# Modulating in place in PSUM, Newton steps with scalar operands, and the residual's affine step from the last tile on

## The chip, the cores and the metric

The kernel runs on one core of one Trainium2 chip. Its engines work side by side, each through its own queue of instructions in a fixed order: PE (TensorE) does matmuls and transposes into PSUM, DVE (VectorE) and ACT (ScalarE) work element by element on SBUF and PSUM, POOL (GpSimd) does element work on SBUF and issues some DMAs, and SP (SyncE) issues most DMAs. The metric is the device time of one execution in microseconds (us); less is better.

## The reference, cut to what matters

Two layers run over 640 tokens of width 1024: 512 latent tokens and 128 context tokens. Each layer is

```python
shift1, scale1, gate1, shift2, scale2, gate2 = jnp.split(mod.astype(x.dtype), 6, axis=-1)
u = x * (1 + scale1) + shift1
q_c, kv_c, k_r, p_in, g_b, g_c, h_in = split_cols(u @ w_in, IN_SIZES)
...   # latent attention, pooling mixer, gated convolution
mix = jnp.concatenate([a_out, b_out, c_out], axis=-1) @ w_out
x = layer_norm(ALPHA * x + gate1 * mix, ln1_g, ln1_b)
u = x * (1 + scale2) + shift2
x = layer_norm(ALPHA * x + gate2 * expert_choice_ffn(u, w_router, w_gate, w_up, w_down), ln2_g, ln2_b)
```

`layer_norm` takes mean and variance over the 1024 columns of a token. The last line of layer 0 and the first three of layer 1 are the boundary that most of this change is about.

## The kernel before, in words

**Tiles.** The tokens are five tiles of 128 rows: t = 0 to 3 latent, t = 4 (`CTX`) context. Weights are read from HBM in float32; a float32 product is made of three matmuls (`mm3`, lines 229 to 232: high by high, high by low, low by high), so every operand is first split into a high part, rounded by a CAST on ACT (`...h`), and a low part, the difference, made on DVE or POOL (`...l`): `split`, lines 225 to 227.

**Stages.** Layer 0: adaLN modulation, combined input projection (column groups A, B, P, GC, H, GB, which accumulate in the PSUM tiles `ps_a`, `ps_b` and `ps_c`), attention and the other mixers, output projection, layer norm, routing, 16 experts in pairs, layer norm; then layer 1 the same. The experts read 6 MB of weights each.

**The boundary between the layers** (`finish`, line 1444 on, called for each tile in turn). A tile's sum stands in two PSUM halves `ps_z`. `ln_stats` takes bn_stats of both halves (L312) and their aggregate (L300); then 1/sqrt(variance + eps) is made. With `dve` true that is `rsqrt_dve`: a first guess by integer arithmetic and three Newton steps, each one `tensor_scalar` (L295) and one `scalar_tensor_tensor` (L296), all on 128x1 values on DVE. With `dve` false it is `rsqrt`: one `tensor_scalar` on DVE (L284) and one power on POOL (L285). Before, all five tiles of the boundary take the Newton form. Then DVE makes `nb` = -mean times that value (L1450), and ACT writes the normalised tile `z` from PSUM in two activations (L1452).

`build_uT` turns `z` into the next layer's input: in two halves g = 0, 1, PE transposes four 128x128 blocks into one PSUM bank `tr8` (L253; two such banks exist, pool `ptr`), `modulate` multiplies and adds per partition, two slices of four on DVE (L264) and two on ACT (L261), into an SBUF tile `umod`, and `split` makes `uTh` (CAST, L226) and `uTl` (difference, L227) of `umod`. The A and B projections of layer 1 multiply `uTh` and `uTl`.

`keep` (line 1472) then turns each `z` into the residual that layer 1 needs later: POOL multiplies by `ln_g` and adds `ln_b` (`affine`, L337 and L338) in place, and issues the store to `xres` (L1477). These are put behind `following["split"]`, a split of weights, in the order of issue.

**What sets the order.** The program is written stage by stage, and a list scheduler orders the instructions of each engine by its own model of times; `tc.issue_after(x)` puts what follows behind x in that order, and `tc.high_priority()` ahead of the rest. So an edit in one place can move rows of an engine far from it. On the chip each engine then follows its own list in order: an instruction whose inputs are late holds back all that stand behind it.

The same `build_uT` starts layer 0 with the tiles of x, with `umod` in the `xhalf` tiles; `zero_pads` uses one more such tile.

## Time and profile before

| | |
|---|---|
| median of three runs | 1296.16 us (1294.45, 1296.16, 1302.5) |
| the profiled execution | 1294.52 us |
| its span (first to last instruction) | 1292.7 us |
| PE busy | 1193.2 us, 92% of the span |
| DVE, ACT, POOL busy | 543.7, 368.3, 252.8 us |
| mean granted TensorE clock | 0.966 |

The profiled execution lies 1.64 us under the median, and 1.8 us of it lie outside its span. A timeline row gives the start of an instruction, its length, its engine, line, operation and tiles, and in brackets how long the engine was idle before it and what ended that. A row "x8" puts eight instructions together. Matmuls are pipelined: a row's length is longer than its distance to the next.

### The profile page before, as it was taken

The numbers are of one execution on the slowest core, as the hardware profiler recorded it, in microseconds if no ns is written. First come the engines' busy times: TensorE is split into PE (matmuls) and PEld (weight loads), VectorE is DVE, ScalarE is ACT, GpSimd is POOL, SyncE is SP. The second block draws the span as 40 slices with busy tenths as digits, with TensorE's granted clock in tenths as the row PEclk, the third lists the DMA queues.
The fourth block names the chain that finished last, engine by engine and source line by source line (L and its number), as shares of the span: only waits on it lengthen the run. The fifth ranks groups of instructions, "written<-read, shape, count | busy, mean of one in ns | idle before, by whom it ended". The sixth has DMA issues, their size and how long they took to land.

```text
span 1292.7 us, 18180 instructions
## 1 busy us (share of the span) xinstructions
PE 1193.2 (92%) x7244; PEld 710.7 (55%) x7244; DVE 543.7 (42%) x1266; ACT 368.3 (28%) x800; POOL 252.8 (20%) x234
## 2 busy tenths in 40 slices
PE   5999999999879999999969999999987999999994
PEld 1877886987523333333349998798752333333331
DVE  1554464777531121111297756477653111111116
ACT  1532134663411110111145423475341101011111
POOL 0210002004330221121175000200433022012114
PEclk8999999999979999999989999999998999999998
DMA  9868666164869999999543315606487999999932
GB/s 360 310 209 301 226 237 226 69 214 150 339 259 402 397 396 406 410 400 332 193 138 98 86 46 197 242 19 225 157 320 287 406 396 396 410 406 386 357 102 82
DMA packets 85078, 342.34 MB, mean 265 GB/s; under 512 B 18713, under 2 KB 32089, under 8 KB 54401
## 3 DMA queue, kind: packets, MB, share of 16 engines
q1 hardware_dynamic: 73568, 305.96, 61.4%
q0 software_dynamic: 9840, 29.45, 8.4%
q10 hardware_dynamic: 1584, 5.77, 1.1%
q8 instruction: 57, 0.93, 0.3%
q14 instruction: 29, 0.23, 0.1%
HBM read 313.73 MB, written 27.51 MB: 264 GB/s over the span
## 4 chain that ended last, share of the span: by engine, by line
PE 84%; DVE 7%; ACT 4%; DMA 2%; issue 1%; SPq 1%; POOL 0%; POOLq 0%; ACTq 0%; DVEq 0%
PE ps_d L239 9%; PE ps_g L239 9%; PE ps_u L239 9%; PE ps_gc L239 8%; PE ps_dc L239 5%; PE ps_ada L185 4%; PE ps_c L230 3%; PE ps_c L232 3%; PE ps_c L231 3%; PE ps_o L231 3%; PE ps_o L230 3%; PE ps_o L232 3%; PE ps_p L733 1%; PE tr L239 1%; PE ps_b L230 1%
## 5 line engine op out<-in xcount | busy, mean ns | idle before, releaser
L239 PE MATMUL ps_g<-wg,xT 128*64 128x512 f32 x512 | 116.1, 595 | 0.1
L239 PE MATMUL ps_d<-wd,hT 128*64 128x512 f32 x512 | 113.6, 595 | 2.5 <-DVE yc L1184 1.6
L239 PE MATMUL ps_u<-wu,xT 128*64 128x512 f32 x512 | 115.4, 592 | 0.0
L239 PE MATMUL ps_gc<-wu,xc 128*32 128x512 f32 x512 | 115.0, 595 | 0.0
L239 PE MATMUL ps_gc<-wg,xc 128*32 128x512 f32 x512 | 115.0, 594 | 0.0
L1161 ACT ACTIVATE sc<-ps_gc 32x512 f32<-32x512 f32 x32 | 18.8, 587 | 328.8 <-PE ps_gc L239 299.7
L1163 DVE TENSOR_TENSOR hc<-ps_gc,sc 32x512 f32<-32x512 f32 x32 | 22.0, 688 | 174.9 <-ACT sc L1161 174.8
L239 PEld LDWEIGHTS ps_d<-wd,hT 128*64 128x64 f32 x512 | 35.5, 137 | 78.7 <-issue 75.7
L1110 POOL DMA_INDIRECT yaccc<-yc,csi x28 | 39.8, 1421 | 192.5 <-DVE yc L1184 155.0
L239 PEld LDWEIGHTS ps_g<-wg,xT 128*64 128x64 f32 x512 | 36.0, 137 | 75.1 <-issue 72.7
L239 PEld LDWEIGHTS ps_u<-wu,xT 128*64 128x64 f32 x512 | 37.2, 137 | 72.6 <-issue 71.8
L239 PE MATMUL ps_dc<-wd,hcT 128*32 128x512 f32 x512 | 71.1, 705 | 0.9 <-ACT hcT L1172 0.9
L239 PEld LDWEIGHTS ps_gc<-wg,xc 128*32 128x32 f32 x512 | 29.2, 110 | 75.0 <-issue 73.7
L185 PE MATMUL ps_ada<-wada,cs 128*32 128x512 f32 x368 | 60.1, 630 | 4.8 <-DMA wada<-in_w_ada_dram 4.8
L1212 DVE SCALAR_TENSOR_TENSOR ye<-ps_d,lg,gl 128x512 f32<-128x512 f32 x32 | 24.0, 751 | 95.7 <-PE ps_d L239 92.9
L1191 DVE TENSOR_TENSOR h<-ps_u,sg 128x512 f32<-128x512 f32 x16 | 11.1, 692 | 104.1 <-PE ps_u L239 104.1
L261 ACT ACTIVATE xT<-tr,modB,modA 128x128 f32<-128x128 f32 x64 | 28.0, 459 | 60.8 <-DVE xT L264 59.1
L239 PEld LDWEIGHTS ps_dc<-wd,hcT 128*32 128x32 f32 x512 | 17.2, 126 | 43.0 <-issue 39.1
L961 POOL DMA_INDIRECT xsl<-zrow,lgi x16 | 15.9, 991 | 102.3 <-PE tr L239 87.9
L285 POOL TENSOR_TENSOR bsd<-bsd,neg_half 128x1 f32<-128x1 f32 x15 | 9.5, 634 | 128.7 <-DVE bsd L284 128.7
L1184 DVE SCALAR_TENSOR_TENSOR yc<-ps_dc,cg,gc 128x512 f32<-128x512 f32 x16 | 12.0, 749 | 52.9 <-PE ps_dc L239 52.9
L227 POOL TENSOR_TENSOR wo00l<-r_wo,wo00h 128x1024 fp32r<-128x1024 f32 x4 | 10.4, 2610 | 119.4 <-ACT wo00h L226 119.4
(618 smaller groups left out, 2839.0 us busy)
## 6 DMA issues: line engine op xcount, KB each, us to landing
wg<-in_w_gate_dram SPq DMA_DIRECT2D x64, 1024.0 KB, 12.4
wu<-in_w_up_dram SPq DMA_DIRECT2D x64, 1024.0 KB, 14.9
wd<-in_w_down_dram SPq DMA_DIRECT2D x64, 1024.0 KB, 17.8
wada<-in_w_ada_dram SPq DMA_DIRECT2D x46, 1024.0 KB, 7.2
r_wo<-in_w_out_dram SPq DMA_DIRECT2D x8, 1024.0 KB, 8.7
zrow<-xa ACTq DMA_DIRECT2D x8, 512.0 KB, 7.7
yacc<-xa POOLq DMA_DIRECT2D x8, 512.0 KB, 9.9
z<-yacc SPq DMA_DIRECT2D x8, 512.0 KB, 6.2
```

Source lines behind the costliest of these rows:

```text
L185: nc.tensor.matmul(ps[32 * j:32 * j + 32, :], lhsT=cs[:, k, :], rhs=w[:, j * 512:(j + 1) * 512], start=(k == 0), stop=(k == KD - 1))
L230: nc.tensor.matmul(out, lhsT=lh, rhs=rh, start=first, stop=False)
L231: nc.tensor.matmul(out, lhsT=lh, rhs=rl, start=False, stop=False)
L232: nc.tensor.matmul(out, lhsT=ll, rhs=rh, start=False, stop=last)
L239: line["pe"] = op(*args, **kw)
L261: nc.scalar.activation(out=out[:, kk, :], in_=ps[:, kk, :], func=AF.Identity, scale=A[:, r, k:k + 1], bias=B[:, r, k:k + 1])
L733: nc.tensor.transpose(pt[:, kk, i * P:(i + 1) * P], prs[i][:, (k0 + kk) * P:(k0 + kk + 1) * P], ident)
L961: ins = nc.gpsimd.indirect_dma_start(out=x, out_offset=None, in_=src, in_offset=bass.IndirectOffsetOnAxis(ap=idx, axis=0))
L1110: nc.gpsimd.indirect_dma_start(out=acc[:, :], out_offset=bass.IndirectOffsetOnAxis(ap=idx[h][0:64, j:j + 1], axis=0), in_=y[hs], in_offset ...
L1161: nc.scalar.activation(out=sc[64 * i + 32:64 * i + 64], in_=pc[64 * i:64 * i + 32], func=AF.Silu)
L1163: nc.vector.tensor_tensor(out=hc[32 * i:32 * i + 32], in0=pc[64 * i + 32:64 * i + 64], in1=sc[64 * i + 32:64 * i + 64], op=ALU.mult)
L1212: order["ye"] = nc.vector.scalar_tensor_tensor(out=ye[:, hs], in0=pd, scalar=lg[:, j:j + 1], in1=gl2[:, hs], op0=ALU.mult, op1=ALU.mult)
```

## The change

`build_uT` has no `umod` tile any more: `modulate` writes in place in the PSUM bank that the transposes filled, and `split` reads that bank. A bank is thus held until its `uTl` is made. Between the layers the second half gives three slices of four to ACT and one to DVE. The Newton step and `nb` become `tensor_scalar` with scalar operands. Tiles 2, 3 and 4 of the boundary take the power on POOL. `keep` runs from the last tile to the first, each tile behind the store of the one before it.

```diff
--- before.py
+++ after.py
@@ -264,15 +264,14 @@
                 nc.vector.tensor_scalar(out=out[:, kk, :], in0=ps[:, kk, :], scalar1=A[:, r, k:k + 1],
                                         scalar2=B[:, r, k:k + 1], op0=ALU.mult, op1=ALU.add)
 
-    def build_uT(t, xn, uTh, uTl, A, B, newhalf, ready=None):
+    def build_uT(t, xn, uTh, uTl, A, B, ready=None, on_act=((1, 3), (1, 3))):
         r = 1 if t == CTX else 0
 
         def emit(g, ps):
             ks = slice(4 * g, 4 * g + 4)
-            u = newhalf("umod").rearrange("p (k n) -> p k n", k=4)
-            modulate(u, ps, A, B, r, g)
+            modulate(ps, ps, A, B, r, g, on_act[g])
             tok = slice(t * P, (t + 1) * P)
-            split(uTh[:, ks, tok], uTl[:, ks, tok], u)
+            split(uTh[:, ks, tok], uTl[:, ks, tok], ps)
         if ready is None:
             transpose8(xn, emit)
         else:
@@ -293,7 +292,7 @@
         nc.vector.tensor_scalar(out=y.bitcast(I32), in0=xe.bitcast(I32), scalar1=-0.5, scalar2=0x5f3759df, op0=ALU.mult, op1=ALU.add)
         for _ in range(3):
             nc.vector.tensor_scalar(out=t, in0=y, scalar1=y[:, 0:1], scalar2=xh, op0=ALU.mult, op1=ALU.mult)
-            nc.vector.scalar_tensor_tensor(out=y, in0=t, scalar=1.5, in1=y, op0=ALU.add, op1=ALU.mult)
+            nc.vector.tensor_scalar(out=y, in0=t, scalar1=1.5, scalar2=y[:, 0:1], op0=ALU.add, op1=ALU.mult)
 
     def ln_final(stt, dve):
         mv = st([P, 2], "bmv")
@@ -319,7 +318,7 @@
                                     op0=ALU.subtract, op1=ALU.mult)
         else:
             nb = st([P, 1], "bnb")
-            nc.vector.scalar_tensor_tensor(out=nb, in0=mv[:, 0:1], scalar=-1.0, in1=sd, op0=ALU.mult, op1=ALU.mult)
+            nc.vector.tensor_scalar(out=nb, in0=mv[:, 0:1], scalar1=sd[:, 0:1], scalar2=-1.0, op0=ALU.mult, op1=ALU.mult)
             nc.scalar.activation(out=z, in_=z, func=AF.Identity, scale=sd[:, 0:1], bias=nb[:, 0:1])
 
     def xin(t):
@@ -1406,9 +1405,9 @@
     for t in range(NT):
         if t == 0:
             with tc.high_priority():
-                build_uT(t, x0, *mp[4], A, B, xhalf, early)
+                build_uT(t, x0, *mp[4], A, B, early)
         else:
-            build_uT(t, xin0(t), *mp[4], A, B, xhalf)
+            build_uT(t, xin0(t), *mp[4], A, B)
     cpool("psf")
     with tc.issue_after(order["u"].ins):
         load_tables()
@@ -1444,14 +1443,14 @@
         def finish(t, ps, L2, newrow, newhalf):
             z = newrow("z", "crow" if t == CTX else "row")
             with tc.high_priority() if l + 1 == depth else ExitStack():
-                mv, sd = ln_stats(ps, l + 1 < depth)
+                mv, sd = ln_stats(ps, l + 1 < depth and t < 2)
             if l + 1 < depth or t < 3:
                 nb = st([P, 1], "bnb")
-                nc.vector.scalar_tensor_tensor(out=nb, in0=mv[:, 0:1], scalar=-1.0, in1=sd, op0=ALU.mult, op1=ALU.mult)
+                nc.vector.tensor_scalar(out=nb, in0=mv[:, 0:1], scalar1=sd[:, 0:1], scalar2=-1.0, op0=ALU.mult, op1=ALU.mult)
                 for n in range(2):
                     nc.scalar.activation(out=z[:, n * 512:n * 512 + 512], in_=ps[n], func=AF.Identity, scale=sd[:, 0:1], bias=nb[:, 0:1])
             if l + 1 < depth:
-                build_uT(t, z, *following["mp"][4], *following["AB"], newhalf)
+                build_uT(t, z, *following["mp"][4], *following["AB"], on_act=((1, 3), (1, 2, 3)))
                 following["z"].append((t, z))
             else:
                 c = 640
@@ -1471,10 +1470,11 @@
 
         def keep(L2):
 
-            for t, z in following["z"]:
-                with tc.issue_after(following["split"].ins):
+            prev = following["split"] if following["z"] else None
+            for t, z in following["z"][::-1]:
+                with tc.issue_after(prev.ins):
                     affine(L2, z, z)
-                nc.gpsimd.dma_start(out=xres[t * P:(t + 1) * P, :], in_=z)
+                    prev = nc.gpsimd.dma_start(out=xres[t * P:(t + 1) * P, :], in_=z)
 
         experts(l, A, B, ctxr, ln, gates, newrow, newhalf, late, xc, route_late, ps_dn, preload, start_next, finish, keep)
         if l + 1 < depth:
```

Three places show how rows move. First PE, where the transposes of tile 1 (`z_5294`) and tile 2 (`z_5347`) meet the first matmuls of layer 1's projection A for tile 0 (`ps_a_5569`). Before:

```order
L253 MATMUL tr8_5315<-ident_72,z_5294 128x128 x4
L253 MATMUL tr8_5327<-ident_72,z_5294 128x128 x4
L253 MATMUL tr8_5368<-ident_72,z_5347 128x128 x4
L253 MATMUL tr8_5380<-ident_72,z_5347 128x128 x4
L230 MATMUL ps_a_5569<-wA10h_5219,uTh1_5217 128x384
L231 MATMUL ps_a_5569<-wA10l_5220,uTh1_5217 128x384
```

After (line numbers of the changed file, one lower from `rsqrt` on), with tile 1 as `z_5282` and tile 0's sum as `ps_a_5525`:

```order
L253 MATMUL tr8_5303<-ident_72,z_5282 128x128 x4
L253 MATMUL tr8_5314<-ident_72,z_5282 128x128 x4
L230 MATMUL ps_a_5525<-wA10h_5209,uTh1_5207 128x384
L231 MATMUL ps_a_5525<-wA10l_5210,uTh1_5207 128x384
L232 MATMUL ps_a_5525<-wA10h_5209,uTl1_5208 128x384
L230 MATMUL ps_a_5525<-wA10h_5209,uTh1_5207 128x384
```

Tile 2's transposes are gone from between tile 1's and the projection. They stand two matmuls into tile 1's sum `ps_a_5564`, `z_5333` being tile 2:

```order
L232 MATMUL ps_a_5525<-wA11h_5215,uTl1_5208 128x384
L230 MATMUL ps_a_5564<-wA10h_5209,uTh1_5207 128x384
L231 MATMUL ps_a_5564<-wA10l_5210,uTh1_5207 128x384
L253 MATMUL tr8_5346<-ident_72,z_5333 128x128 x4
L232 MATMUL ps_a_5564<-wA10h_5209,uTl1_5208 128x384
```

So 26 matmuls stand ahead of the first transposes of tile 2 that before stood behind them.

Second POOL, from the first affine step on. Before, with `z_5249` as tile 0, `z_5294` tile 1, `z_5347` tile 2 and `z_5400` tile 3 (`rs` are the scales of layer 1's latent norms, six of which come later):

```order
L337 TENSOR_TENSOR z_5249<-z_5249,ln2_g_0_4099 128x1024
L338 TENSOR_TENSOR z_5249<-z_5249,ln2_b_0_4102 128x1024
L1477 DMA xres_97<-z_5249 128x1024
L337 TENSOR_TENSOR z_5294<-z_5294,ln2_g_0_4099 128x1024
L338 TENSOR_TENSOR z_5294<-z_5294,ln2_b_0_4102 128x1024
L1477 DMA xres_97<-z_5294 128x1024
L337 TENSOR_TENSOR z_5347<-z_5347,ln2_g_0_4099 128x1024
L338 TENSOR_TENSOR z_5347<-z_5347,ln2_b_0_4102 128x1024
L1477 DMA xres_97<-z_5347 128x1024
L337 TENSOR_TENSOR z_5400<-z_5400,ln2_g_0_4099 128x1024
L285 TENSOR_TENSOR rs_5597<-rs_5597,neg_half_77 128x1
L338 TENSOR_TENSOR z_5400<-z_5400,ln2_b_0_4102 128x1024
```

After, with `z_5417` as tile 4, `z_5376` tile 3 and `z_5333` tile 2; tiles 1 and 0 follow, and then the clearing of the pooling mixer's `pext`:

```order
L284 TENSOR_TENSOR rs_5631<-rs_5631,neg_half_77 128x1
L336 TENSOR_TENSOR z_5417<-z_5417,ln2_g_0_4089 128x1024
L337 TENSOR_TENSOR z_5417<-z_5417,ln2_b_0_4092 128x1024
L284 TENSOR_TENSOR rs_5670<-rs_5670,neg_half_77 128x1
L1477 DMA xres_97<-z_5417 128x1024
L336 TENSOR_TENSOR z_5376<-z_5376,ln2_g_0_4089 128x1024
L284 TENSOR_TENSOR rs_5709<-rs_5709,neg_half_77 128x1
L337 TENSOR_TENSOR z_5376<-z_5376,ln2_b_0_4092 128x1024
L1477 DMA xres_97<-z_5376 128x1024
L336 TENSOR_TENSOR z_5333<-z_5333,ln2_g_0_4089 128x1024
L284 TENSOR_TENSOR rs_5764<-rs_5764,neg_half_77 128x1
L284 TENSOR_TENSOR rs_5815<-rs_5815,neg_half_77 128x1
```

The affine steps have moved behind the scales of the first three tiles, and the scales of the others now stand between them.

Third DVE at the statistics of tiles 2 and 3. Before, the last Newton steps of both (`bsd_5353`, `bsd_5406`), between them a `uTl`:

```order
L296 SCALAR_TENSOR_TENSOR bsd_5353<-nw_5354,bsd_5353 128x1
L296 SCALAR_TENSOR_TENSOR bsd_5406<-nw_5407,bsd_5406 128x1
L295 TENSOR_SCALAR nw_5354<-bsd_5353,nw_5354 128x1
L295 TENSOR_SCALAR nw_5407<-bsd_5406,nw_5407 128x1
L296 SCALAR_TENSOR_TENSOR bsd_5353<-nw_5354,bsd_5353 128x1
L227 TENSOR_TENSOR uTl1_5218<-umod_5320,uTh1_5217 128x4x128
L296 SCALAR_TENSOR_TENSOR bsd_5406<-nw_5407,bsd_5406 128x1
L1450 SCALAR_TENSOR_TENSOR bnb_5364<-bmv_5351,bsd_5353 128x1
L1450 SCALAR_TENSOR_TENSOR bnb_5417<-bmv_5404,bsd_5406 128x1
L300 BN_AGGR bmv_5455<-bst_5452 128x2
L227 TENSOR_TENSOR uTl1_5218<-umod_5332,uTh1_5217 128x4x128
```

After, the same two tiles, to the second `nb` (`bsd_5339`, `bsd_5382`), whose power is on POOL:

```order
L299 BN_AGGR bmv_5337<-bst_5334 128x2
L299 BN_AGGR bmv_5380<-bst_5377 128x2
L283 TENSOR_SCALAR bsd_5339<-bmv_5337 128x1
L311 BN_STATS bst_5418<-ps_z_5411 128x6
L283 TENSOR_SCALAR bsd_5382<-bmv_5380 128x1
L1449 TENSOR_SCALAR bnb_5342<-bmv_5337,bsd_5339 128x1
L1449 TENSOR_SCALAR bnb_5385<-bmv_5380,bsd_5382 128x1
L311 BN_STATS bst_5418<-ps_z_5414 128x6
```

The Newton rows are gone; one row (L283) comes ahead of POOL and one (L1449) behind it.

Off the boundary: at layer 0's start the zeroing of the `zt` tile, and the store that uses it, come earlier, and the scheduler orders much of both layers' projections anew (PE 4547 rows before, 4544 after); the experts stay nearly as they were. On the SP queue the loads `qnb`, `knb`, `cck` and `ckr` of layer 1 wait before for the last `uTl`, since their memory was that of `umod`; after, they don't.

## Rows read from the trace of the kernel before

**Rows 1.** The page, part 1 (busy time of each engine) and part 4 (chain that ended last).

```profile
PE 1193.2 (92%) x7244; PEld 710.7 (55%) x7244; DVE 543.7 (42%) x1266; ACT 368.3 (28%) x800; POOL 252.8 (20%) x234
...
PE 84%; DVE 7%; ACT 4%; DMA 2%; issue 1%; SPq 1%; POOL 0%; POOLq 0%; ACTq 0%; DVEq 0%
```

**Rows 2.** Windows: us, length, busy us of each engine, granted clock (PEclk), DMA share, GB/s.

```profile
664.00:674.00 10.00, 0.65 (x3) 0.65 (x4) 9.51 (x33) 4.33 (x9) 7.37 (x5) 0.60 0.51 190
720.00:820.00 100.00, 100.00 (x655) 92.93 (x654) 58.28 (x120) 36.07 (x82) 1.97 (x14) 1.00 0.38 127
1020.00:1220.00 200.00, 192.70 (x1154) 66.56 (x1148) 35.50 (x63) 24.84 (x54) 33.16 (x25) 0.97 1.02 396
```

**Rows 3.** Timeline of PE at the boundary: start us, length us, instruction, idle time before it.

```profile
653.99 0.75 PE L253 MATMUL tr<-ident,z 128*128 128x128 f32 x4 [0.57 <-ACT z L1452]
662.44 1.12 PE L253 MATMUL tr<-ident,z 128*128 128x128 f32 x8
673.36 1.98 PE L253 MATMUL tr<-ident,z 128*128 128x128 f32 x8 [9.79 <-ACT z L1452]
674.99 0.67 PE L230 MATMUL ps_a<-wA10h,uTh 128*128 128x384 f32 x1
...
676.53 0.34 PE L232 MATMUL ps_a<-wA10h,uTl 128*128 128x384 f32 x1
679.68 1.13 PE L253 MATMUL tr<-ident,z 128*128 128x128 f32 x8
...
682.08 0.45 PE L230 MATMUL ps_a<-wA10h,uTh 128*128 128x384 f32 x1 [1.10 <-ACT z L1452]
```

**Rows 4.** Timeline of PE, a little later.

```profile
699.93 0.44 PE L421 MATMUL ps_ck<-ident,cck 128*128 128x128 f32 x2 [1.14 <-DMA cck<-in_cache_ckv_dram]
```

**Rows 5.** Lines by form: count, ns min/median/max, first and last start us, shapes.

```profile
L296 DVE SCALAR_TENSOR_TENSOR bsd<-nw,bsd x15: 146/160/2183, 647.4 to 678.6; 128x1 f32<-128x1 f32 x15
L295 DVE TENSOR_SCALAR nw<-bsd,nw x15: 257/266/276, 647.1 to 678.1; 128x1 f32<-128x1 f32 x15
L227 DVE TENSOR_TENSOR uTl<-umod,uTh x20: 640/693/2879, 33.9 to 694.0; 128x512 fp32r<-128x512 f32 x20
L859 DVE TENSOR_TENSOR ps_o<-ps_o,gate x20: 679/700/700, 281.6 to 951.1; 128x512 f32<-128x512 f32 x20
L264 DVE TENSOR_SCALAR umod<-tr,modA,modB x20: 394/402/411, 655.3 to 691.1; 128x128 f32<-128x128 f32 x20
L261 ACT ACTIVATE umod<-tr,modB,modA x20: 448/457/474, 657.3 to 692.2; 128x128 f32<-128x128 f32 x20
L226 ACT CAST uTh<-umod x20: 609/619/622, 33.2 to 692.7; 128x512 fp32r<-128x512 f32 x20
L337 POOL TENSOR_TENSOR z<-z,ln_g x5: 2364/2386/2812, 659.9 to 691.1; 128x1024 f32<-128x1024 f32 x5
L285 POOL TENSOR_TENSOR bsd<-bsd,neg_half x15: 544/563/1125, 295.7 to 1280.4; 128x1 f32<-128x1 f32 x15
```

**Rows 6.** Timeline of DVE over the same stretch.

```profile
650.89 1.44 DVE L296 SCALAR_TENSOR_TENSOR bsd<-nw,bsd 128x1 f32<-128x1 f32 x1
...
652.98 0.14 DVE L1450 SCALAR_TENSOR_TENSOR bnb<-bmv,bsd 128x1 f32<-128x1 f32 x1
...
660.69 2.56 DVE L227 TENSOR_TENSOR uTl<-umod,uTh 128x512 fp32r<-128x512 f32 x1 [0.21 <-ACT uTh L226]
...
672.34 0.28 DVE L1450 SCALAR_TENSOR_TENSOR bnb<-bmv,bsd 128x1 f32<-128x1 f32 x2
```

**Rows 7.** Timeline of POOL.

```profile
648.71 3.60 POOL L227 TENSOR_TENSOR wA11l<-r_wA,wA11h 128x768 fp32r<-128x768 f32 x2
```

**Rows 8.** Timelines of ACT and of the SP queue.

```profile
653.15 3.03 ACT L1452 ACTIVATE z<-ps_z,bnb,bsd 128x512 f32<-128x512 f32 x4 [4.42 <-DVE bnb L1450]
...
694.06 0.34 SPq L222 DMA_DIRECT2D qnb<-in_q_norm_dram  x1
```

**Rows 9.** Timeline of DVE at layer 0's start.

```profile
33.92 1.24 DVE L227 TENSOR_TENSOR uTl<-umod,uTh 128x512 fp32r<-128x512 f32 x1
```

## The prediction

> **What bounds the kernel now.** I read the page first, then the windows for the place where the busiest engine is not busy, then the timelines there. The page says that PE is busy for 92% of the span and makes 84% of the chain that ended last, with DVE 7% [rows 1]: a faster DVE is worth something only where PE stands still for it. The windows find one such place that this change touches. From 664 to 674 us PE worked 0.65 of 10 us while DVE worked 9.51 [rows 2]; that is the boundary between the layers. Fifty microseconds later PE is busy for 100.00 of 100 us [rows 2], so time won at the boundary is kept there, not swallowed by another wait.
>
> The PE timeline shows four stops at the boundary: 0.57, 9.79 and 1.10 us, all ended by ACT's normalisation of a tile, and 1.14 us, ended by the load `cck` [rows 3, 4]. Sum 12.60 us. After the long stop PE is also slower: the granted clock over 664 to 674 was 0.60 [rows 2], the eight transposes at 673.36 took 1.98 us where those at 662.44 took 1.12, and six matmuls from 674.99 to 676.53 took 1.54 us, where the 18 from there to 679.68 took 0.175 each, so 1.05 for six [rows 3]. That is 0.86 + 0.49 = 1.35 us more, from a clock between its levels of 1.2 and 2.4 GHz. So 13.95 us are there to be won.
>
> The long stop has one cause in the order: tile 2's transposes stand ahead of all matmuls of the projection, though only they need tile 2's statistics. Those come late because DVE's own work is held up. L296 takes 0.16 us in the median and up to 2.18; L227 on `uTl` 0.69 and up to 2.88 [rows 5]. One L296 begins at 650.89 and ends at 652.33, where a pair of POOL instructions ends (648.71 + 3.60 = 652.31) [rows 6, 7]. Both take two inputs from SBUF. L295, with the same 128x1 values under the same POOL work, has one SBUF input as a stream and stays within 257 and 276 ns [rows 5]; L859 and L264, which read PSUM, stay within 700 and 411 [rows 5].
>
> **The change, part by part.**
>
> *Newton with scalars.* Six L296 (tiles 0 and 1) become `tensor_scalar`; nearest row L295, 0.27 us each [rows 5]. A single hold, 1.44 instead of 0.27, is 1.17 us; the first stop is 0.57. Tile 0's `nb`, now at 652.98 [rows 6], comes at least 1.2 earlier, so the stop goes: +0.57. PE then runs on from 653.42.
>
> The Trainium skill says the opposite could hold: by "SBUF — State Buffer", section "Who interferes with whom", `tensor_scalar` can enter a mode that uses both port pairs, and then contends with POOL as a two-input instruction does. By that rule the new rows would be held as L296 was; L295's fifteen rows here disagree for 128x1, so the sum doesn't use it.
>
> *Power on POOL for tiles 2 to 4.* It removes 27 DVE instructions of 0.14 to 0.27 us, some of them held, and adds three scalings on DVE and three POOL rows of 0.56 (up to 1.13) [rows 5]. POOL has its split of `wB10l` there, then nothing, as the affine steps have moved away: the power waits for nobody.
>
> *Modulation in PSUM.* `uTl` has one SBUF input, so I take 0.69 always. Tile 0's second `uTl` before ended at 663.25 after 2.56 us [rows 6]; now about 661.4. In-place writing: no row shows ACT or `tensor_scalar` doing it in PSUM. The nearest, L859 on DVE in place in PSUM, is 0.70 at 512 columns, beside 0.69 for an unheld `uTl` in SBUF [rows 5]: bounds 0 and 0.01 each, forty times, 0.4 us if all lay on the path. A gain is as far away. I take 0.
>
> *The order.* Tile 1's transposes ended at 663.56 [rows 3], now at 663.0, and tile 0's projection follows at once, where it began at 674.99. It takes 24 x 0.175 = 4.2 us, to 667.2. Now tile 1 is late. ACT has the normalisation of tiles 2, 3 and 4 ahead of most of its slices: six activations of 3.03 / 4 = 0.76 [rows 8], 4.5 us. They can start when tile 2's power is there: behind tile 0's `uTl` at 661.4, 0.14 for the scaling, 0.56 for the power, 0.14 for `nb`, so 662.2, and end at 666.8. Then three slices of 0.46 and the CAST of 0.62 [rows 5], at 668.8; with one hand-over to DVE, 0.40, 669.2. PE waits 2.0 us, then 0.35 more before its third matmul, for `uTl` (0.69 less two matmuls). That is 2.35 us of new stop.
>
> From there PE has more work than the others for each tile: 4.2 + 1.12 for a projection and transposes, plus 12 `ps_b` matmuls (320 of 384 columns, so 0.146 each, an estimate: 1.75) for two of the tiles. For DVE it is 3 slices and 2 `uTl`, 2.6 us; for ACT 5 slices and 2 CASTs, 3.5 us, plus a square sum. So no stop of 1.10 at tile 3: the stops of 9.79 and 1.10 go. The wait of 1.14 for `cck` goes too: its load was issued behind `qnb` at 694.06 [rows 8], which waited for the memory of `umod`; now nothing holds these four loads.
>
> *The affine steps.* Ten POOL instructions of 2.39 us [rows 5] and five issues, from 659.9 to 697 before, now begin behind tile 4, at about 690, and end near 720. There DVE splits `wB11`, `wP10`, `wP11` and turns the rotary keys, all two-input in SBUF. A hold can cost up to 2.39. PE has `ps_b` matmuls in hand, so most are covered. I take 1.3 us, about half of one hold, between 0 and three holds (7.2).
>
> *Layer 0.* The first `uTl`, for which PE's third matmul waits, took 1.24 us [rows 9] instead of 0.69, so I take +0.5, between -1 (adaLN matmuls placed earlier may meet their load) and +1.
>
> *The experts and the tail* keep their rows; the `nb` of the last tiles changes by under 0.2 us.
>
> **Sum**: 12.60 + 1.35 - 2.35 - 1.3 + 0.5 = 10.8 us. The profiled execution of 1294.52 would become 1283.7. It lies 1.64 under the median of the three runs, so for the median, 1296.16 - 10.8 = 1285.4, and I say **1285**.
>
> **The rivals.**
>
> *The banks are too few.* Two `tr8` banks are now held through the split. If the two halves of a tile don't overlap, a half takes 0.40 + 0.46 + 0.40 + 0.46 + 0.62 + 0.69 = 3.0 us, a tile with its transposes 7.1, against PE's 7.05 with `ps_b` and 5.3 without. Two tiles with 0.1 and two with 1.8 are 3.8 us: 1289. For it: an engine was often waiting for the other's slice. Against: the halves overlap in the order of DVE and ACT.
>
> *The late affine steps hold DVE at the wrong time.* Three holds on PE's path in place of the 1.3: 7.2 - 1.3 = 5.9 us back, 1291. For it: L296 and `uTl` were held in just this way; against: PE's `ps_b` work.
>
> *The experts take it back.* From 1020 to 1220 the DMA share is 1.02 at 396 GB/s and PE busy 192.70 of 200 [rows 2]. If the weights' stream there did not start earlier with the rest, the gain would be spent waiting for it: 1296. Against: buffers come free as PE gets on, so the stream shifts with it.
>
> *Newton's new form is held like the old.* Then the first stop stays, 0.57: 1286.
>
> *Slower.* Six scales of the latent norms now stand between affine steps on POOL's queue, in order. If each waits for one 2.39 us step and PE waits for each, that is 14.3 us: 1285.4 + 14.3 = 1300. It decides from 10.8 / 6 = 1.8 us for each on. Against: PE has most of `ps_b` and `ps_c` to do, with nothing from POOL.
>
> **How the numbers follow.** Chances: forecast 0.60 (1281 to 1289), banks 0.11, affine 0.12, experts 0.06, Newton 0.06, slower 0.05. The low end: no new stop at tile 1, no hold, +1 in layer 0, so 13.95 + 1 = 15 us, 1281; with 1 us for the scatter of the runs 1280. The high end takes in banks and affine with the same 1 us and some more: 1294. Above it lie the experts and slower (0.11), below it some 0.07. About 1%, 13 us, is what a measurement of this kernel can tell from no change. Faster by that means under 1283.2: a good part of the forecast's own range, 0.24. Slower by that needs over 1309, twice nearly the price of the slower rival: 0.03. Within 1%: 0.73.
>
> **What would show it.** Right: PE's long stop before tile 2's transposes gone, a stop of about 2 us behind tile 0's projection, no clock of 0.60 there, every `tensor_scalar` Newton row under 0.3 us, `uTl` always near 0.69, `cck` not waited for, and the first of the 100% windows 10 to 12 us earlier. Wrong: stops of over 2 us before each pair of transposes (banks), long rotary or split rows at 695 to 725 with PE waiting (affine), the shift shrinking between 720 and 1260 us (experts), or layer 0's end moved by more than 1 us.

## The result and the profile after

The changed kernel takes 1284.56 us (median of four runs, 1282.19 to 1288.32) where the kernel before took 1295.9 in the same job: 11.3 us less, a ratio of 0.9908 with a 95% interval of 0.9879 to 0.9937. In a second job it took 1284.85 against 1298.33, 0.9901 (0.9879 to 0.9922). The forecast was 1285 with a range of 1280 to 1294. The profiled execution of the changed kernel took 1288.32 us, its span is 1286.5; it is the longest of its four runs, so the comparison of the two spans, 6.2 us, shows less than the medians do. Why, is in the part on the clock below.

The page, parts 1 and 4, of the changed kernel. Since [rows 1] PE's busy share has risen from 92% to 93%, and DVE's share of the chain has fallen from 7% to 4%:

```profile
PE 1196.0 (93%) x7244; PEld 708.7 (55%) x7244; DVE 524.0 (41%) x1237; ACT 367.9 (29%) x805; POOL 254.5 (20%) x237
...
PE 83%; DVE 4%; ACT 3%; DMA 3%; issue 2%; POOL 2%; SPq 1%; POOLq 0%; ACTq 0%; DVEq 0%
```

The windows at the boundary (start and end in us, length, busy us of PE, PEld, DVE, ACT and POOL with counts, granted clock, DMA share, GB/s). Where PE worked 0.65 of 10 us at a clock of 0.60 [rows 2], it now works 19.28 of 20 at 1.00:

```profile
640.00:660.00 20.00, 20.00 (x111) 8.75 (x107) 12.68 (x37) 10.18 (x16) 10.09 (x6) 1.00 0.32 102
660.00:680.00 20.00, 19.28 (x100) 15.85 (x99) 11.70 (x31) 13.62 (x30) 2.89 (x6) 1.00 0.38 106
680.00:700.00 20.00, 20.00 (x129) 19.92 (x128) 11.27 (x21) 11.28 (x27) 9.35 (x7) 1.00 0.07 27
700.00:720.00 20.00, 19.05 (x133) 18.52 (x132) 16.49 (x39) 8.81 (x31) 16.97 (x13) 1.00 0.44 136
```

The PE timeline there, to be read against [rows 3]. The transposes of tile 0 and 1 have no stop ahead of them, tile 0's projection begins right behind with a stop of 0.60 us, and tile 1's begins 4.27 us later without one:

```profile
657.11 0.75 PE L253 MATMUL tr<-ident,z 128*128 128x128 f32 x4
...
665.58 1.12 PE L253 MATMUL tr<-ident,z 128*128 128x128 f32 x8
667.31 0.44 PE L230 MATMUL ps_a<-wA10h,uTh 128*128 128x384 f32 x1 [0.60 <-ACT z L1451]
...
671.58 0.41 PE L230 MATMUL ps_a<-wA10h,uTh 128*128 128x384 f32 x1
```

All that is left behind that, up to the scores, are two late stops; the one for `cck` [rows 4] is gone:

```profile
714.67 0.42 PE L232 MATMUL ps_c<-uTh,wP11l 128*128 128x320 f32 x1 [0.46 <-DVE wP11l L227]
...
721.00 0.41 PE L420 MATMUL ps_ck<-ident,ckn 128*128 128x128 f32 x2 [1.49 <-DVE kr L400]
```

The lines by form, against [rows 5]. The Newton step's second half takes 0.20 to 0.21 us, always; `uTl` never more than 0.694; writing in place in PSUM costs DVE 0.418 instead of 0.402 and saves ACT a little, 0.431 instead of 0.457, and the CAST from PSUM takes 0.586 instead of 0.619:

```profile
L294 DVE TENSOR_SCALAR nw<-bsd,nw x6: 257/272/276, 651.6 to 655.4; 128x1 f32<-128x1 f32 x6
...
L295 DVE TENSOR_SCALAR bsd<-nw,bsd x6: 196/212/214, 652.4 to 655.7; 128x1 f32<-128x1 f32 x6
...
L227 DVE TENSOR_TENSOR uTl<-tr,uTh x20: 674/691/694, 34.8 to 692.4; 128x512 fp32r<-128x512 f32 x20
...
L264 DVE TENSOR_SCALAR tr<-tr,modA,modB x15: 368/418/420, 657.9 to 689.5; 128x128 f32<-128x128 f32 x15
...
L261 ACT ACTIVATE tr<-tr,modB,modA x25: 421/431/482, 658.8 to 690.9; 128x128 f32<-128x128 f32 x25
...
L226 ACT CAST uTh<-tr x20: 578/586/659, 34.0 to 691.8; 128x512 fp32r<-128x512 f32 x20
```

**A measure for the boundary.** The whole time scatters by several us from execution to execution, so the experiments are read by one stretch as well: from the start of the first `ps_z` matmul of layer 0's end to the start of the last score matmul `scc` of layer 1. In the kernel before:

```profile
L239 PE MATMUL ps_z<-z,ident x16: 591/592/697, 642.1 to 1262.3; 128*128 128x512 f32 x16
...
L689 PE MATMUL scc<-kh,qh x8: 222/266/327, 221.7 to 854.7; 128*128 128x128 f32 x8
```

That is 854.7 - 642.1 = 212.6 us. In the changed kernel:

```profile
L239 PE MATMUL ps_z<-z,ident x16: 590/592/697, 645.9 to 1256.0; 128*128 128x512 f32 x16
...
L688 PE MATMUL scc<-kh,qh x8: 222/264/327, 222.4 to 846.4; 128*128 128x128 f32 x8
```

846.4 - 645.9 = 200.5 us, and 200.4 in the second profile: 12.1 us less.

Not all of that is the boundary's. From the first to the last of these score matmuls of layer 1 it is 22.8 us in the kernel before (831.9 to 854.7) and 21.3 in the changed one (825.2 to 846.4). Both have the same two stops there, 0.90 and 0.45 us, but the granted clock from 820 to 840 us was 0.91 in the one and 1.00 in the other. Two profiles of one and the same kernel, no_keep and no_keep_b below, differ in just this way, so it is chance and not the change (windows of before, no_keep and no_keep_b):

```profile
820.00:840.00 20.00, 18.65 (x114) 12.95 (x113) 10.37 (x23) 9.89 (x18) 7.00 (x4) 0.91 0.76 283
...
820.00:840.00 20.00, 18.64 (x143) 17.39 (x136) 14.18 (x43) 14.21 (x35) 1.80 (x2) 1.00 0.60 229
...
820.00:840.00 20.00, 18.64 (x126) 16.92 (x125) 12.68 (x36) 11.71 (x28) 4.54 (x3) 0.91 0.75 285
```

Of the fourteen profiles, four have this late slow clock and take 22.8 to 22.9 us there: before, only_newton, no_newton and no_keep_b. The other ten take 21.2 to 21.3. Less these 1.6 us, the stretch before is 211.0 us, and the boundary gave 10.5.

### The profile page after: what moved, and what is told of

The parts are those of the page before. It is cut to its first block, busy times and chain, and to the rows that moved or that the text cites. A ratio compares the mean times of both kernels' runs of the same rounds, so it can differ in the third digit from the quotient of the medians.

```text
span 1286.5 us, 18175 instructions
## 1 busy us (share of the span) xinstructions
PE 1196.0 (93%) x7244; PEld 708.7 (55%) x7244; DVE 524.0 (41%) x1237; ACT 367.9 (29%) x805; POOL 254.5 (20%) x237
## 4 chain that ended last, share of the span: by engine, by line
PE 83%; DVE 4%; ACT 3%; DMA 3%; issue 2%; POOL 2%; SPq 1%; POOLq 0%; ACTq 0%; DVEq 0%
PE ps_d L239 9%; PE ps_g L239 8%; PE ps_u L239 8%; PE ps_gc L239 8%; PE ps_dc L239 5%; PE ps_ada L185 4%; PE ps_c L230 3%; PE ps_o L230 3%; PE ps_o L231 3%; PE ps_o L232 3%; PE ps_c L232 3%; PE ps_c L231 3%; PE ps_p L732 1%; DMA ln_b<-in_ln_b_dram 1%; PE ps_a L230 1%
## 5 line engine op out<-in xcount | busy, mean ns | idle before, releaser
L239 PE MATMUL ps_d<-wd,hT 128*64 128x512 f32 x512 | 117.5, 613 | 0.9 <-ACT hT L1198 0.9
L1109 POOL DMA_INDIRECT yacc<-ye,lgi x14 | 19.9, 1422 | 84.0 <-DVE ye L1211 74.1
```

Source lines behind the costliest of these rows:

```text
L239: line["pe"] = op(*args, **kw)
L1109: nc.gpsimd.indirect_dma_start(out=acc[:, :], out_offset=bass.IndirectOffsetOnAxis(ap=idx[h][0:64, j:j + 1], axis=0), in_=y[hs], in_offset ...
```

## Experiments

The kernels with one part of the change alone are named only_, those with one part undone no_. Stretch as defined, in brackets without the late slow clock of 1.6 us where a profile has it; "stops" are PE's idle times of over 0.4 us from the boundary's transposes to 760 us; "clock" is the lowest granted clock among the three windows of 20 us that begin 20 us behind the stretch's start, so a fall behind those 60 us isn't in the column. The kernel before had a median of 1297.96 us in the job of the four only_, 1295.76 in that of the first four no_, and 1298.33 in the last. The ratios are those on record, each against the kernel before of the same job; they differ from the quotients of the medians by up to 0.2%. The expectations were written with the uncorrected stretch.

| kernel | median us | ratio to before (95%) | stretch us | stops us | clock |
|---|---|---|---|---|---|
| before | 1295.9 | | 212.6 (211.0) | 0.57, 9.79, 1.10, 1.14 | 0.74 |
| changed | 1284.56 | 0.9908 (0.9879 to 0.9937) | 200.5 | 0.60, 0.46, 1.49 | 1.00 |
| only_pow | 1293.07 | 0.9978 (0.9963 to 0.9993) | 212.2 | 0.57, 6.82, 2.66 | 0.74 |
| only_keep | 1296.57 | 1.0006 (0.9988 to 1.0024) | 209.5 | 0.55, 4.78, 1.04, 1.51, 1.30, 0.77 | 0.83 |
| only_newton | 1290.2 | 0.9951 (0.9936 to 0.9967) | 208.2 (206.6) | 7.53 | 0.74 |
| only_psum | 1290.87 | 0.9946 (0.9930 to 0.9963) | 207.7 | 8.15, 0.58 | 0.74 |
| no_keep | 1281.9 | 0.9886 (0.9858 to 0.9914) | 200.7 | 2.44 | 0.91 |
| no_newton | 1286.01 | 0.9914 (0.9890 to 0.9938) | 205.2 (203.6) | 2.61, 0.45, 1.49 | 0.91 |
| no_psum | 1294.22 | 0.9974 (0.9957 to 0.9992) | 206.8 | 2.44, 0.98, 1.94 | 0.83 |
| no_pow | 1296.34 | 1.0000 (0.9984 to 1.0016) | 208.8 | 3.81, 1.94, 1.46 | 0.83 |
| again | 1284.85 | 0.9901 (0.9879 to 0.9922) | 200.4 | 0.60, 0.47, 1.48 | 1.00 |
| no_keep_b | 1283.18 | 0.9889 (0.9869 to 0.9909) | 202.3 (200.7) | 2.44 | 0.91 |
| mid | 1285.26 | 0.9899 (0.9870 to 0.9928) | 197.7 | 0.61 | 1.00 |
| quarter | 1286.77 | 0.9924 (0.9903 to 0.9945) | 205.2 | 0.60, 1.76, 1.49, 1.83 | 1.00 |

**only_pow**: the order alone.

```diff
-                mv, sd = ln_stats(ps, l + 1 < depth)
+                mv, sd = ln_stats(ps, l + 1 < depth and t < 2)
```

> Only the power on POOL for tiles 2 to 4 is added to the kernel before; the scheduler then puts tile 2's transposes behind tile 0's projection. Theory 'order' (the long stop is there because tile 2's transposes stand ahead of the projection): the 9.79 us stop goes, PE starts the projection at about 664 instead of 675, and the stretch from the first ps_z to the last scores of layer 1 (212.6 us before, 200.5 after) falls to about 204; uTl is still held by POOL up to 2.9 us, so new stops of 1 to 3 us in all stay. Time about 8 us under before. Theory 'holds' (the stop is there because POOL holds DVE): the holds are all still there, so at most 4 us are won.

The scheduler did what the changed kernel shows: tile 2's transposes stand behind tile 0's projection. Yet the stretch is 212.2 us, 0.4 under before, and 1.2 over it without the late clock. PE's stop has moved to the head of the projection and others have come behind (PE timeline):

```profile
669.79 0.69 PE L230 MATMUL ps_a<-wA10h,uTh 128*128 128x384 f32 x1 [6.82 <-ACT z L1452]
...
696.51 0.69 PE L232 MATMUL ps_a<-wA10h,uTl 128*128 128x384 f32 x1 [2.66 <-DVE uTl L227]
```

DVE shows why (timeline): `uTl` is held as before, and now `nb`, a 128x1 instruction of 0.14 us, is held for 2.99 and 2.33 us by the affine steps that run beside it. The first of these two is tile 3's. It ends at 668.92, 0.03 us behind an affine step of POOL (666.53 + 2.36, POOL timeline); ACT then normalises the first half of tile 3 until 669.73 (ACT timeline), and there PE's stop ends. Tile 2's `nb`, at 665.49, was not held; why the projection waits for tile 3 is told further below:

```profile
660.09 2.56 DVE L227 TENSOR_TENSOR uTl<-umod,uTh 128x512 fp32r<-128x512 f32 x1 [0.21 <-ACT uTh L226]
...
665.93 2.99 DVE L1450 SCALAR_TENSOR_TENSOR bnb<-bmv,bsd 128x1 f32<-128x1 f32 x1
...
670.36 2.33 DVE L1450 SCALAR_TENSOR_TENSOR bnb<-bmv,bsd 128x1 f32<-128x1 f32 x1 [0.74 <-POOL bsd L285]
```

Theory "order" is out in the form that the prediction gave it. "Holds" allowed up to 4 us; in the stretch even that did not come. The whole time did fall, by 2.9 us (0.9978, 0.9963 to 0.9993); no row of the boundary shows where, so that stays open.

**only_keep**: the affine steps alone, late and from the last tile on.

```diff
-            for t, z in following["z"]:
-                with tc.issue_after(following["split"].ins):
+            prev = following["split"] if following["z"] else None
+            for t, z in following["z"][::-1]:
+                with tc.issue_after(prev.ins):
                     affine(L2, z, z)
+                    prev = nc.gpsimd.dma_start(...)
```

> Only the affine steps are moved behind the last split of the boundary, from the last tile on. Theory 'order': tile 2's transposes still stand ahead of the projection, and tile 2's Newton steps come without the holds of 2.15 and 1.48 us and the uTl hold of 1.9 us, so the long stop falls from 9.8 to about 5 us; 4 to 5 us won. Theory 'holds': the holds are what costs, the stop falls below 2 us and 8 us or more are won.

The long stop fell to 4.78 us, as "order" said, but four new ones of 0.77 to 1.51 us came where the affine steps now lie, each ended by a two-input DVE row or by one behind it (PE timeline; one of the four is shown). 3.1 us of the stretch are won, 1.5 without the late clock; the whole time shows none of it:

```profile
671.28 1.98 PE L253 MATMUL tr<-ident,z 128*128 128x128 f32 x8 [4.78 <-ACT z L1452]
...
714.69 0.44 PE L421 MATMUL ps_ck<-ident,ckn 128*128 128x128 f32 x2 [1.30 <-DVE qcl L227]
```

**only_newton**: the scalar operands alone.

```diff
-            nc.vector.scalar_tensor_tensor(out=y, in0=t, scalar=1.5, in1=y, op0=ALU.add, op1=ALU.mult)
+            nc.vector.tensor_scalar(out=y, in0=t, scalar1=1.5, scalar2=y[:, 0:1], op0=ALU.add, op1=ALU.mult)
...
-            nc.vector.scalar_tensor_tensor(out=nb, in0=mv[:, 0:1], scalar=-1.0, in1=sd, op0=ALU.mult, op1=ALU.mult)
+            nc.vector.tensor_scalar(out=nb, in0=mv[:, 0:1], scalar1=sd[:, 0:1], scalar2=-1.0, op0=ALU.mult, op1=ALU.mult)
```

> Only the Newton step and nb take scalar operands. By the rule that tensor_scalar can be held like a two-input instruction L296's rows stay up to 2 us and nothing is won. By L295's rows they take 0.2 to 0.3 us always. Theory 'order': tile 2 is still ahead of the projection; its statistics come about 4 us earlier, the long stop falls to 5 or 6 us; 4 us won, less what uTl is then held more. Theory 'holds': 6 us or more.

The edit stands at the other `nb` line too. No step is held any more (line by form), beside the same POOL work that held it before:

```profile
L296 DVE TENSOR_SCALAR bsd<-nw,bsd x15: 202/208/215, 649.1 to 675.4; 128x1 f32<-128x1 f32 x15
```

But what came free is partly held one instruction later: the two `uTl` of tile 0 now take 5.23 us together (DVE timeline), and tile 2's transposes still wait (PE timeline). 4.4 us of the stretch are won; both profiles have the late clock:

```profile
659.69 5.23 DVE L227 TENSOR_TENSOR uTl<-umod,uTh 128x512 fp32r<-128x512 f32 x2
```

```profile
672.16 1.98 PE L253 MATMUL tr<-ident,z 128*128 128x128 f32 x8 [7.53 <-ACT z L1452]
```

**only_psum**: the modulation in place alone, with `on_act`.

```diff
-            u = newhalf("umod").rearrange("p (k n) -> p k n", k=4)
-            modulate(u, ps, A, B, r, g)
+            modulate(ps, ps, A, B, r, g, on_act[g])
...
-            split(uTh[:, ks, tok], uTl[:, ks, tok], u)
+            split(uTh[:, ks, tok], uTl[:, ks, tok], ps)
```

> Only the modulation is in place in PSUM, with three of four slices of the second half on ACT. uTl always takes about 0.69 us. The four loads qnb, knb, cck, ckr come earlier, so the 1.14 us stop goes. Theory 'order': the long stop shrinks only by the hold of one uTl, 1.9 us; 2 to 3 us won in all. Theory 'banks' (holding a bank through the split costs PE): new stops of 1 to 2 us at each tile, nothing won or a loss.

4.9 us of the stretch and 7 of the time, more than either theory said; without the late clock it is 3.3 us of the stretch, just over what "order" said. The long stop is still 8.15 us, as the Newton steps are still held (DVE timeline; two steps together took 2.95 us). The stops of 1 to 2 us at each tile that "banks" said did not come: one of 0.58 is left behind the long one, ended by ACT's normalisation. The long stop itself ends, by its row, with DVE. What the transposes need of DVE is the bank, which a `uTl` of tile 1 reads until 674.00 (DVE timeline); the half of `z` that they turn is there at 674.02 (ACT timeline). So bank and `z` came together, and what the bank alone would cost is not shown.

```profile
674.15 1.95 PE L253 MATMUL tr<-ident,z 128*128 128x128 f32 x8 [8.15 <-DVE nw L290]
```

```profile
667.17 2.95 DVE L295 SCALAR_TENSOR_TENSOR bsd<-nw,bsd 128x1 f32<-128x1 f32 x2
```

**no_keep**: the affine steps back where they were.

```diff
-            prev = following["split"] if following["z"] else None
-            for t, z in following["z"][::-1]:
-                with tc.issue_after(prev.ins):
+            for t, z in following["z"]:
+                with tc.issue_after(following["split"].ins):
```

> The changed kernel with the affine steps left where they were, from the first tile on and early. The measure is the stretch from the first ps_z to the last scores of layer 1: 212.6 us before, 200.5 changed. Theory 'additive' (each edit is worth what it was worth alone: affine 3.1, Newton 4.4, PSUM 4.9, power 0.4 us): 203.6. Theory 'together' (each edit takes one two-input DVE instruction out of POOL's way, and the gain comes when none is left on tile 0's to 2's chain): without the affine move nothing on the chain can be held any more, only the power of tile 2 queues about 1 us behind tile 0's affine step, while the late stops of 0.46 and 1.49 us go: 200 to 201.

200.7 us, as "together" said: with the other three edits nothing on the chain has two inputs in SBUF, and early affine steps hold nobody. The two late stops are gone. The stop ahead of the projection is 2.44 instead of 0.60 (PE timeline), and the rows show two reasons. The power of tile 2 waits on POOL's queue for tile 0's affine step, 0.65 us from when its input is there (660.39) to 661.04 (POOL timeline). And DVE's list has changed: tile 4's second bn_stats, which waits for PE, now stands ahead of tile 2's `nb` (DVE timeline). The power is done at 661.61, `nb` comes at 662.58; in the changed kernel `nb` stands ahead of that bn_stats and follows its power by 0.03 us (664.85, 664.89):

```profile
665.33 0.44 PE L230 MATMUL ps_a<-wA10h,uTh 128*128 128x384 f32 x1 [2.44 <-ACT z L1451]
```

```profile
658.72 2.36 POOL L337 TENSOR_TENSOR z<-z,ln_b 128x1024 f32<-128x1024 f32 x1
661.04 1.10 POOL L284 TENSOR_TENSOR bsd<-bsd,neg_half 128x1 f32<-128x1 f32 x2
```

```profile
661.97 0.70 DVE L311 BATCH_NORM_STATS2 bst<-ps_z 128x6 f32<-128x512 f32 x1 [0.92 <-PE ps_z L1291]
662.58 0.20 DVE L1449 TENSOR_SCALAR bnb<-bmv,bsd 128x1 f32<-128x1 f32 x1
```

Its time is 1281.9 and, in no_keep_b, 1283.18, beside 1284.56 and 1284.85 for the changed kernel; the intervals overlap. So this part of the change brought nothing; that it costs is not shown.

**no_newton**: the two-input Newton step and `nb` back (the diff of only_newton reversed).

> The changed kernel with the two-input Newton step and nb. Additive: 204.9. Together: two-input rows stand only at tiles 0 and 1 (six Newton steps, held by the weight splits on POOL) and in five nb; POOL has nothing else while tile 2's nb is made, so only the first stop of 0.57 and up to 1 us behind it come back: 201 to 202.

205.2 looks near to "additive" (204.9), but 1.6 us of it are the late clock; without it it is 203.6, between the two theories. Its stops are 2.0 us longer in all than the changed kernel's, the first one 2.61 (PE timeline), and the clock fell to 0.91 over the 20 us behind that stop. No DVE row at the statistics of tiles 2 and 3 is held there: the `nb` take 0.14 and 0.15 us, and POOL has only the powers to do. What differs is DVE's list: tile 3's second bn_stats now stands behind tile 0's second `uTl` and not ahead of it, and tile 4's second one ahead of tile 2's `nb` (663.32, where the power was done at 662.80). So this cost comes at least in part from the order that the scheduler made anew; what the hold of 1.44 us on a Newton step of tile 0 or 1 (at 650.01) adds is not separated from it:

```profile
666.01 0.44 PE L230 MATMUL ps_a<-wA10h,uTh 128*128 128x384 f32 x1 [2.61 <-ACT z L1451]
```

**no_psum**: `umod` back, two slices each on ACT and DVE (the diff of only_psum reversed).

> The changed kernel with umod in SBUF and two slices each on ACT and DVE. Additive: 205.4. Together: uTl of tile 0 is held by the split of wB10l until about 660, the later ones by the power alone; the loads qnb to cck wait for the last uTl again (1.1 us); ACT and DVE hand over more often: 202 to 203.

206.8, worse than both. Tile 0's two `uTl` before the projection are not held (0.69 us each); tile 4's second bn_stats stands ahead of tile 2's `nb` here too, and the stop ahead of the projection is 2.44. Two stops of 0.98 and 1.94 come late, both for the rotary key `kr` on DVE (PE timeline; the second is shown), whose two-input rows `rp` took 2.17 and 2.37 us beside late affine steps. The clock fell twice, to 0.91 and 0.83:

```profile
715.68 0.48 PE L422 MATMUL ps_ck<-ident,kr 128*128 128x128 f32 x1 [1.94 <-DVE kr L401]
```

**no_pow**: Newton on DVE for all tiles (the diff of only_pow reversed).

> The changed kernel with Newton steps on DVE for all five tiles. The scheduler then puts the first half of tile 2's transposes ahead of tile 0's projection again. Additive: 200.9. Together, with the order: tile 2's first half waits for its Newton steps, unheld but among two tiles' work on DVE: a stop of 3 to 5 us is back, 204 to 206.

208.8: without the power the other three parts are worth 3.8 us of the stretch, 2.2 without the late clock, and nothing in time. The stop of 3.81 stands at the first half of tile 2's transposes (PE timeline), and two more follow. It ends with a `uTl` of tile 1 (DVE timeline, 665.84 + 0.69 = 666.53), so the transposes waited for the bank that this `uTl` reads. The half of `z` that they turn was there at 666.48 (ACT timeline), hardly earlier:

```profile
666.68 1.10 PE L253 MATMUL tr<-ident,z 128*128 128x128 f32 x4 [3.81 <-DVE uTl L227]
```

```profile
665.84 0.69 DVE L227 TENSOR_TENSOR uTl<-tr,uTh 128x512 fp32r<-128x512 f32 x1 [0.29 <-ACT uTh L226]
```

**again**, **no_keep_b**, **mid** and **quarter** ran side by side. The first two are the changed kernel and no_keep once more.

> The changed kernel once more, on the same chip as the three others. Stops at the boundary of 0.60, 0.46 and 1.49 us and a stretch of 200.5 us as before, whatever the whole time is; if the profiled execution's time differs from 1288.3, the difference lies in the two expert stages (about 270 or 273.5 us from the first ps_g to the first ps_z, 262 or 266 from layer 1's routing to its last ps_g).

> The changed kernel with the early affine steps once more, on the same chip: a stop of 2.44 us ahead of the projection, none later, stretch 200.7; time within 1 us of the changed kernel's if both sides cost the same (1.95 against 1.84 us).

Stops as before in both. no_keep_b's stretch is 202.3, 1.6 longer than no_keep's with the same stops: that is the late slow clock.

**mid**: the affine steps from the first tile on, behind the last power. `order["pow"]` is that power; the store is issued as in the kernel before.

```diff
-                with tc.issue_after(following["split"].ins):
+                with tc.issue_after(order["pow"].ins):
```

> The changed kernel with the affine steps from the first tile on, put behind the power of tile 4. Theory 'two sides': late affine steps cost the stops of 0.46 and 1.49 us behind 714, early ones (no_keep) put tile 2's power behind tile 0's affine step and so lengthen the stop ahead of the projection from 0.60 to 2.44 us. Here neither should be: stop of 0.60 ahead of the projection, none later, the stretch from the first ps_z to the last scores about 198.7 us against 200.5 and 200.7; time 1.8 us under both. Rival (the affine steps hold DVE wherever they lie): stops of 1 us or more show up at tiles 1 to 4, stretch 200 or more.

Both sides are avoided: one stop of 0.61 in the whole boundary (PE timeline), and the rotary rows are never held (line by form; up to 2.19 us in the changed kernel). DVE's list has tile 2's `nb` ahead of tile 4's second bn_stats, as in the changed kernel, so no_keep's two reasons are both gone and not told apart. The stretch is 197.7, 2.8 us shorter than the changed kernel's. In the whole time it can't be told: 1285.26 as median, from 1279.8, the lowest run of all, to 1288.77.

```profile
667.19 0.45 PE L230 MATMUL ps_a<-wA10h,uTh 128*128 128x384 f32 x1 [0.61 <-ACT z L1451]
```

```profile
L400 DVE TENSOR_TENSOR kr<-rp,rp x16: 215/219/226, 77.8 to 714.7; 128x64 f32<-128x64 f32 x16
```

**quarter**: each late affine instruction in four pieces.

```diff
-                    affine(L2, z, z)
+                    for n in range(4):
+                        cols = slice(n * 256, n * 256 + 256)
+                        affine({k: v[:, cols] for k, v in L2.items()}, z[:, cols], z[:, cols])
```

> The changed kernel with each late affine instruction cut into four of 256 columns. If a hold lasts as long as the one POOL instruction that is running, no DVE row is held for more than 0.7 us and the stops of 0.46 and 1.49 us shrink to 0.5 us or less in all. If POOL keeps DVE out as long as it has work, the rows stay at 2 us or more and the stops stay.

Smaller pieces made the holds longer. One DVE row lasts 5.10 us (DVE timeline). Seven POOL pieces stand there one behind the other without a gap, from 710.69 to 715.57 (POOL timeline); the DVE row ends 0.55 us behind them, which is about its own time:

```profile
711.02 5.10 DVE L227 TENSOR_TENSOR wP11l<-r_wP,wP11h 128x512 fp32r<-128x512 f32 x1
```

```profile
710.69 2.82 POOL L336 TENSOR_TENSOR z<-z,ln_g 128x256 f32<-128x256 f32 x4
713.48 2.09 POOL L337 TENSOR_TENSOR z<-z,ln_b 128x256 f32<-128x256 f32 x3
```

The same happened to `wB11l`, beside eight pieces (691.62 to 697.18), and cost the stop of 1.76. So in both places the held DVE instruction came in when POOL had a gap, not when one piece ended. A third stop, 1.83 us, ended by ACT's `pext`, was not followed up. With whole instructions there is a gap of 0.08 us between the multiplication and the addition, which needs its result (659.88 + 2.81 = 662.69 and 662.77 in the kernel before, where `uTl` came in, to end at 663.25); four pieces of the one kind need nothing of each other. That the gap is what lets DVE in is read from these rows; no kernel with a gap between pieces was run.

## Why the prediction was right, and where it was not

**The time and the sum.** 1284.56 against 1285. The four stops and the slow clock were there to be won, as the working said: 12.60 us of stops became 2.55, and the granted clock is 1.00 from 640 to 720. By terms:

- *First stop, +0.57*: gone. *Long stop, +9.79*, and *tile 3's, +1.10*: gone. *`cck`, +1.14*: gone. Right.
- *New stop, -2.35, behind tile 0's projection*: wrong in place and size. It stands ahead of that projection and takes 0.60. The working had PE start as soon as `uTl` was there. In fact the PSUM bank of the first `ps_a` was one of the `ps_z`, and that comes free when ACT has normalised its tile: the row says that `z` on L1451 ended the stop, and in the program the wait is for the first half of tile 3. In the trace that half ends at 667.25 and PE starts at 667.31; in only_pow, no_keep and no_newton the two lie 0.05 us apart as well. In exchange, tile 1's projection waited for nothing: the four activations for tiles 2 and 3 took 2.78 us, 0.70 each, and no hand-over came between ACT's three last slices.
- *Late affine steps, -1.3*: 0.46 + 1.49 = 1.95 in stops, and 2.8 by mid, which has none of them and the shorter stretch; the mechanism is the one named. `wP11l` took 3.13 us and `kr` 2.19 (DVE timeline); the affine instructions beside them end at 714.05 and 720.57 (POOL timeline), 0.56 and 0.09 us ahead of them:

```profile
711.48 3.13 DVE L227 TENSOR_TENSOR wP11l<-r_wP,wP11h 128x512 fp32r<-128x512 f32 x1
...
718.47 2.19 DVE L400 TENSOR_TENSOR kr<-rp,rp 128x64 f32<-128x64 f32 x1
```

```profile
711.63 2.42 POOL L336 TENSOR_TENSOR z<-z,ln_g 128x1024 f32<-128x1024 f32 x1
...
718.14 2.43 POOL L337 TENSOR_TENSOR z<-z,ln_b 128x1024 f32<-128x1024 f32 x1
```

- *Layer 0, +0.5*: 0.5 to 1.1 in the mean, with ranges that overlap. The first score matmul of layer 0 stands at 220.2 to 222.4 us in the nine profiles with the PSUM edit (mean 220.9) and at 221.2 to 223.2 in the five without (mean 222.0); the first expert matmul `ps_g` stands at 372.0 to 373.6 (mean 372.5) and at 371.7 to 375.1 (mean 373.1).
- Sum of what was forecast for the boundary: 12.60 + 1.35 - 2.35 - 1.3 = 10.3; measured 10.5 without the late clock, which is also what the sum gives with these two sizes (12.60 + 1.35 - 0.60 - 2.8; the 1.35 of clock as forecast). With layer 0 it is 11.0 to 11.6; the medians show 11.3. That the sum is so near is partly luck: the new stop cost 1.75 us less than forecast and the late affine steps 1.5 more, and the two cancel.
- One sign did not come: a shift of 10 to 12 us behind the boundary. The last score matmul of layer 1 stands 8.3 us earlier (854.7, 846.4), as the first `ps_z` stands 3.8 later (642.1, 645.9) behind the experts of layer 0.

**The cause: a step that failed.** "The long stop has one cause in the order", said the prediction, and then took its whole size for the order's term. only_pow has that order and wins 0.4 us. The stop is the end of a chain: `uTl` and `nb`, the Newton steps and the power all must come in time, and in the kernels with one part alone each two-input one among them is seen held by POOL. Without the late clock the four parts alone won -1.2 (power), 1.5 (affine), 4.4 (Newton) and 3.3 us (PSUM), 8.0 in all, where the four together won 10.5. Undone one by one they cost 8.3, 0.2, 3.1 and 6.3. The power is worth nothing alone and most in company; the affine steps the other way round, since the Newton and PSUM parts already take away what early affine steps could hold. So the split of the sum among causes was not right.

How much of each loss is holds is not shown. Each undone edit let the scheduler make a new list, and the 2.44 to 2.61 us ahead of the projection in no_keep, no_newton and no_psum come with an `nb` that stands behind one more bn_stats, and without a held row at tile 2's or 3's statistics. A kernel with one part undone and the order kept would tell the two apart; none was run.

**The rivals.** *Banks*: no transpose stopped PE for over 0.4 us to wait for a bank with `uTl` in the changed kernel. In no_pow one did (3.81 us), and in only_psum (8.15 us) perhaps, but `z` came within 0.05 us of the bank in both. So the stops that this rival foretold did not come here; that two banks always suffice is not shown. *Late affine steps*: this was not a rival but a part of what happened, at 2.8 of its 7.2 us. *Experts take it back*: not shown; their time in layer 0 varies as much in one kernel as between kernels (see below). *Newton held in its new form*: out, by its 15 rows in only_newton, 0.202 to 0.215 us. The Trainium skill's "SBUF — State Buffer", section "Who interferes with whom", names `tensor_scalar` among those that can take the shared ports when their operands meet certain conditions; at 128x1 these rows show no hold. On instructions with two SBUF inputs the trace agrees with it: `nb` as such took up to 2.99 us beside POOL in only_pow. *Slower by six scales on POOL*: none of PE's stops was ended by them.

## What to carry to other kernels

A stop at the end of a chain of small instructions is not owned by one of them: test the parts alone and undone before a cause is named, since a part can be worth nothing alone and 8 us in company, and read the lists of both kernels, since an edit that is undone can also move rows. Beside a busy POOL, try to give each DVE instruction on the path at most one tensor from SBUF (a scalar operand, or a PSUM tile in place): in mid, with POOL's affine steps right behind the powers, one stop of 0.61 us was left. Put such POOL work behind the POOL instructions that are on the path. Read what a PE row waits for through its bank too: the tile that had the bank before may be the last to come.

## What the runs showed of the hardware that I had not expected

**A stop can cost twice.** Where PE stood still for 2.44 us (no_keep), the granted clock over the 20 us from 662.10 on was 0.91 (window):

```profile
662.10:682.10 20.00, 17.56 (x101) 17.37 (x100) 8.84 (x24) 12.69 (x27) 13.14 (x12) 0.91 0.38 125
```

In the changed kernel and mid, with a stop of 0.60 there, it was 1.00 up to 760 us. 9% of 20 us is 1.8 us, an estimate of what the clock adds, not much less than the stop itself. It doesn't follow from the length of the stop alone: in quarter the clock stayed at 1.00 behind the stops of 1.76 and 1.49 us and was 0.91 over the 20 us around that of 1.83 (window), and behind the same stops of 0.90 and 0.45 us at the scores it fell in four profiles and not in ten.

```profile
720.00:740.00 20.00, 18.16 (x116) 17.89 (x115) 10.52 (x23) 6.82 (x20) 8.25 (x21) 0.91 0.56 170
```

**Part of the scatter of the whole time is the clock in the expert stages.** The same 32 matmuls of the first expert's down projection took 9.58 us in the changed kernel's profile, behind a stop of 1.99 us:

```profile
391.24 9.58 PE L239 MATMUL ps_d<-wd,hT 128*64 128x512 f32 x32 [0.46 <-ACT hT L1198]
```

and 7.09 in that of the kernel before, behind one of 1.47:

```profile
390.02 7.09 PE L239 MATMUL ps_d<-wd,hT 128*64 128x512 f32 x32 [0.46 <-ACT hT L1199]
```

(PE timelines; the stops stand ahead of the row before, `ps_hT`, and wait for ACT's `xT`. The granted clock from 380 to 400 us was 0.83 and 1.00.) From the first `ps_g` of layer 0 to its first `ps_z` the profiles show 269.8 to 273.4 us; the kernel no_keep alone shows 269.9 and 273.0. In its second profile these matmuls took 8.34 us behind a stop of 1.52, in its first 7.09 behind one of 1.47. What makes the stop longer and the clock fall in one execution and not in another stays open; it wasn't tried.

**POOL's small pieces keep DVE out longer** than its large ones: 5.10 us in quarter against 3.13 in the changed kernel, for the same `wP11l`: by the rows, a train of pieces without gaps held it like one long instruction.
